# A small projection matrix loaded first, in wider rows on fewer partitions

## The chip, the cores and the metric

The kernel runs on one core of a Trainium2 chip. Times are device microseconds (us) of one execution; a lower time is better. The profile's "span" is what the profiler covers of the same execution; it is some 1.8 us shorter than the time (82.6 against 84.35 us for the kernel before). A run is called slow when it lies over 1.5% above the fastest of the same kernel. Engines: TensorE (PE) multiplies matrices, VectorE (DVE) and GpSimd (POOL) do the elementwise work, ScalarE (ACT) copies and issues DMA, SyncE (SP) only issues DMA.

## The reference

```python
# x: 32 x 512 x 256 f32 (16.8 MB); conditioning: 32 x 64; both projections: 64 x 256
gamma = conditioning @ gamma_proj
beta = conditioning @ beta_proj
return x * (1 + gamma[:, None, :]) + beta[:, None, :]
```

16.8 MB must be read and as much written; gamma and beta need only 136 KB of input.

## The kernel before

x goes through SBUF in four slabs of 4 MB, 32 rows of 1 KB in each of 128 partitions. Each slab is worked on in two pieces of 16 rows: VectorE does 11 rows, GpSimd 5. The small inputs are issued on ACT's queue, x on SP's, the stores on ACT's.

```python
nc.scalar.dma_start(out=cond_s, in_=conditioning)
nc.scalar.dma_start(out=gbproj[:, :dim], in_=gamma_proj)   # 64 partitions, 1 KB rows
nc.scalar.dma_start(out=gbproj[:, dim:], in_=beta_proj)
# SP: slab 0 in two loads (8 and 24 rows), slabs 1 to 3 whole          ...
# cond_T (64 x 512): conditioning transposed, each column 16 times     ...
for s in range(SLABS):
    nc.tensor.matmul(p_t, lhsT=cond_T[:, s*P:(s+1)*P], rhs=gbproj, start=True, stop=True)
    nc.scalar.activation(out=s_t[:, :dim], in_=p_t[:, :dim], ...)      # 1 + gamma, for GpSimd
    nc.scalar.copy(out=s_t[:, dim:], in_=p_t[:, dim:])                 # beta, for GpSimd
for s in range(SLABS):
    for r0 in range(0, ROWS, GROUP):
        # VectorE: v = (gamma + 1) * v, then v + beta; GpSimd: w * gb_s, then w + gb_s   ...
        nc.scalar.dma_start(out=o_v[s, :, r0:r0+GROUP, :], in_=xs[:, r0:r0+GROUP, :])
```

## Time and profile before

| | before |
|---|---|
| time, median of 3 | 84.44 us (84.38 to 84.47) |
| span of the profiled run | 82.6 us |
| conditioning / gamma / beta landed | 3.7 / 10.3 / 14.6 us |
| VectorE's first multiply | 17.5 us |
| first store issued | 25.9 us |
| last load of x landed | 49.5 us |
| VectorE's last operation ends | 66.6 us |
| DMA full | 1.6 to 81.2 us |

A landing time is the issue time plus the "us to landing" of the issue table. Most of the lines behind this table stand in the prediction. Two more follow: the first store in the timeline (start, duration, engine, operation), and the end of the loads among SP's own waits (total, times, longest). SP had issued its last load at 10.6 us, and 38.9 us later x was complete.

```profile
25.94 4.32 ACTq L105 DMA_DIRECT2D out_dram<-xs  x2
...
SPq L132 <- DMA xs<-in_x_dram: 38.9, 1, 38.9
```

### The profile page before, as it was taken

To read this page: it belongs to the slowest core of one execution; us is meant where nothing else is said; L and a number is where in the kernel's file an instruction comes from. 1 tells how busy PE (TensorE), PEld (TensorE's weight loads), DVE (VectorE), ACT (ScalarE), POOL (GpSimd) and SP (SyncE) were. 2 spreads that over 40 slices of the span, in tenths; PEclk is the share of its full clock that TensorE was granted. 3 is DMA by queue.
4 is the path that set the end of the run, shared out by engine and by line. 5 is a ranking of instruction groups with operands and counts; after the bars stand their busy time and mean duration, and the time that the engine had idled before them with its cause. 6 is when DMAs were issued, how large, how long until landed. Compare 5 with 4: busy or idle time off the path is not lost.

```text
span 82.6 us, 156 instructions
## 1 busy us (share of the span) xinstructions
PE 9.1 (11%) x10; PEld 2.8 (3%) x10; DVE 49.9 (60%) x18; ACT 3.9 (5%) x9; POOL 46.2 (56%) x22
## 2 busy tenths in 40 slices
PE   0080000899600000000000000000000000000000
PEld 0100000443000000000000000000000000000000
DVE  2011000059999999999999999999999920000000
ACT  0600000034400000000000000000000000000000
POOL 2000000069999999999999999999995000000000
DMA  3899999969969989998889979899999999999992
GB/s 56 337 508 397 389 397 524 460 302 508 508 270 492 508 381 381 413 476 381 381 381 556 460 302 460 381 468 421 429 452 389 468 421 421 460 389 452 437 421 87
DMA packets 2080, 33.69 MB, mean 408 GB/s; under 512 B 288, under 2 KB 416, under 8 KB 416
## 3 DMA queue, kind: packets, MB, share of 16 engines
q1 hardware_dynamic: 720, 16.78, 48.6%
q10 hardware_dynamic: 1360, 16.92, 48.0%
HBM read 16.92 MB, written 16.78 MB: 408 GB/s over the span
## 4 chain that ended last, share of the span: by engine, by line
DVE 49%; DMA 16%; issue 11%; PE 2%; ACTq 1%; ACT 1%
DVE xs L100 30%; DVE xs L103 19%; DMA gbproj<-in_beta_proj_dram 16%; PE gb_p L79 2%; ACTq L50 1%; ACTq L48 0%; ACT gb_s L82 0%; ACT gb_s L85 0%
## 5 line engine op out<-in xcount | busy, mean ns | idle before, releaser
L102 POOL TENSOR_TENSOR xs<-xs,gb_s 128x1280 f32<-128x1280 f32 x8 | 23.0, 2895 | 16.2 <-ACT gb_s L82 16.2
L100 DVE SCALAR_TENSOR_TENSOR xs<-gb_p,xs 128x2816 f32<-128x2816 f32 x8 | 24.7, 3083 | 10.9 <-ACT gb_s L85 10.9
L103 DVE TENSOR_TENSOR xs<-xs,gb_p 128x2816 f32<-128x2816 f32 x8 | 24.7, 3086 | 0.3
L104 POOL TENSOR_TENSOR xs<-xs,gb_s 128x1280 f32<-128x1280 f32 x8 | 23.0, 2893 | 0.0
L79 PE MATMUL gb_p<-gbproj,cond_T 64*128 64x512 f32 x8 | 7.2, 1074 | 8.9 <-DMA gbproj<-in_beta_proj_dram 8.9
L74 DVE COPY cond_T<-cond_T_p 64x512 f32<-64x512 f32 x1 | 0.7, 683 | 4.3 <-PE cond_T_p L72 4.3
L79 PEld LDWEIGHTS gb_p<-gbproj,cond_T 64*128 64x128 f32 x8 | 2.5, 328 | 13.7 <-issue 13.7
L72 PE MATMUL cond_T_p<-rident,cond_s 32*64 32x512 f32 x2 | 1.9, 1065 | 3.9 <-DMA cond_s<-in_conditioning_dram 3.9
L82 ACT ACTIVATE gb_s<-gb_p 128x256 f32<-128x256 f32 x4 | 1.5, 383 | 16.4 <-PE gb_p L79 16.4
L85 ACT COPY gb_s<-gb_p 128x256 f32<-128x256 f32 x4 | 1.5, 367 | 0.0
L82 ACT ACT_TABLE_LOAD x1 | 1.3, 1283 | 2.4 <-issue 2.4
L67 DVE COPY rident<-ident 32x512 f32<-32x512 f32 x1 | 0.4, 416 | 1.2 <-POOL ident masks.py:199 1.2
L72 PEld LDWEIGHTS cond_T_p<-rident,cond_s 32*64 32x64 f32 x2 | 0.3, 202 | 3.9 <-issue 3.9
masks.py:197 POOL MEMSET ident<- 32x32 f32 x1 | 0.1, 114 | 0.3 <-POOLq L121 0.3
masks.py:199 POOL TENSOR_SCALAR_AFFINE_SELECT ident<-ident 32x32 f32<-32x32 f32 x1 | 0.2, 202 | 0.1
L121 POOL MEMSET const-float32-0.0<- 128x1 f32 x1 | 0.1, 103 | 0.2 <-issue 0.2
L121 POOL MEMSET const-bfloat16-1.0<- 128x1 bf16 x1 | 0.1, 106 | 0.0
L121 POOL MEMSET const-uint8-127<- 128x1 uint8 x1 | 0.1, 106 | 0.0
L121 POOL MEMSET const-float32-1.0<- 128x1 f32 x1 | 0.1, 103 | 0.0
## 6 DMA issues: line engine op xcount, KB each, us to landing
out_dram<-xs ACTq DMA_DIRECT2D x8, 2048.0 KB, 18.2
xs<-in_x_dram SPq DMA_DIRECT2D x3, 4096.0 KB, 32.9
xs<-in_x_dram SPq DMA_DIRECT2D x1, 3072.0 KB, 12.2
xs<-in_x_dram SPq DMA_DIRECT2D x1, 1024.0 KB, 4.6
gbproj<-in_gamma_proj_dram ACTq DMA_DIRECT2D x1, 64.0 KB, 9.1
gbproj<-in_beta_proj_dram ACTq DMA_DIRECT2D x1, 64.0 KB, 12.9
cond_s<-in_conditioning_dram ACTq DMA_DIRECT2D x1, 8.0 KB, 3.0
```

What stands on the lines that cost most here:

```text
L50: nc.scalar.dma_start(out=gbproj[:, :dim], in_=gamma_proj)
L67: nc.vector.tensor_copy(out=rident.rearrange("p (b g) -> p b g", g=REP), in_=ident.to_broadcast([batch, batch, REP]),)
L72: nc.tensor.matmul(cond_T_p, lhsT=cond_s, rhs=rident, start=True, stop=True)
L74: nc.vector.tensor_copy(out=cond_T, in_=cond_T_p)
L79: nc.tensor.matmul(p_t, lhsT=cond_T[:, s * P : (s + 1) * P], rhs=gbproj, start=True, stop=True)
L82: nc.scalar.activation(out=s_t[:, :dim], in_=p_t[:, :dim], func=mybir.ActivationFunctionType.Identity, bias=1.0, scale=1.0)
L85: nc.scalar.copy(out=s_t[:, dim:], in_=p_t[:, dim:])
L100: nc.vector.scalar_tensor_tensor(out=v, in0=rows(g_p, nv), scalar=1.0, in1=v, op0=ALU.add, op1=ALU.mult)
L102: nc.gpsimd.tensor_tensor(out=w, in0=w, in1=rows(g_s, nw), op=ALU.mult)
L103: nc.vector.tensor_add(out=v, in0=v, in1=rows(b_p, nv))
L104: nc.gpsimd.tensor_tensor(out=w, in0=w, in1=rows(b_s, nw), op=ALU.add)
L121: nc = _bacc.Bacc("TRN2", target_bir_lowering=False, num_devices=1)
```

## The change

The intent is an earlier start of VectorE: gamma becomes the first transfer of ACT's queue, as 16 rows of 4 KB and not 64 of 1 KB, with the conditioning and beta behind it. Gamma then lies four rows to a partition, so its product is four accumulated matmuls over 16 partitions, and the conditioning is transposed twice, once for each layout. The elementwise part is also pinned to its written order, so GpSimd no longer does both multiplications of a slab before its additions.

```diff
-    nc.scalar.dma_start(out=cond_s, in_=conditioning)
-    nc.scalar.dma_start(out=gbproj[:, :dim], in_=gamma_proj)
-    nc.scalar.dma_start(out=gbproj[:, dim:], in_=beta_proj)
+    nc.scalar.dma_start(out=gproj, in_=gproj_src)       # "(q j) d -> q j d", 16 x 4 x 256
+    nc.scalar.dma_start(out=cond_s, in_=conditioning)
+    nc.scalar.dma_start(out=bproj, in_=beta_proj)
 ...
-    nc.tensor.matmul(cond_T_p, lhsT=cond_s, rhs=rident, start=True, stop=True)
+    for j in range(CJ):
+        nc.tensor.matmul(cond_T_p[:, j, :], lhsT=cond_s.rearrange("b (q j) -> b j q", j=CJ)[:, j, :],
+                         rhs=ident, start=True, stop=True)
+    nc.tensor.matmul(cond_T_b, lhsT=cond_s, rhs=ident, start=True, stop=True)
 ...   # per slab: two copies that spread the columns, c_t and d_t
-        nc.tensor.matmul(p_t, lhsT=cond_T[:, s * P : (s + 1) * P], rhs=gbproj, start=True, stop=True)
+        for j in range(CJ):
+            nc.tensor.matmul(p_t[:, :dim], lhsT=c_t[:, j, :], rhs=gproj[:, j, :],
+                             start=j == 0, stop=j == CJ - 1)
+        nc.tensor.matmul(p_t[:, dim:], lhsT=d_t, rhs=bproj, start=True, stop=True)
 ...
+    with tc.manual_schedule():
         # the elementwise loop and the stores, as before
```

More of the change, by code (lines that the diff above doesn't have):

```diff
@@ L28 @@
     P = 128
-    SLABS = 4
-    BS = batch // SLABS
-    REP = P // BS
-    ROWS = BS * seq // P
-    assert SLABS * BS == batch and REP * BS == P and ROWS * REP == seq
-    x_v = x.flatten_outer_dims().rearrange("(s p r) d -> s p r d", s=SLABS, p=P)
-    o_v = out.flatten_outer_dims().rearrange("(s p r) d -> s p r d", s=SLABS, p=P)
-    LOADS = {0: [8, 24]}
-    GROUP = 16
-    ON_DVE = 11
+    SLABS = [(8, [8, 24]), (8, [32]), (8, [32]), (8, [32])]
+    assert sum(n for n, _ in SLABS) == batch
+    STORES = [[16, 16], [16, 16], [16, 16], [16, 16]]
+    PIECE, ON_DVE = 16, 11
+    x_f = x.flatten_outer_dims()
+    o_f = out.flatten_outer_dims()
     consts = ctx.enter_context(tc.tile_pool(name="consts", bufs=1))
@@ L44 @@
     psum = ctx.enter_context(tc.tile_pool(name="psum", bufs=1, space=bass.MemoryType.PSUM))
-    cond_s = consts.tile([batch, cond_dim], f32)
-    nc.scalar.dma_start(out=cond_s, in_=conditioning)
-    gbproj = consts.tile([cond_dim, 2 * dim], f32)
-    nc.scalar.dma_start(out=gbproj[:, :dim], in_=gamma_proj)
-    nc.scalar.dma_start(out=gbproj[:, dim:], in_=beta_proj)
-    slabs = []
-    for s in range(SLABS):
-        xs = xpool.tile([P, ROWS, dim], f32, name=f"xs{s}")
-        slabs.append(xs)
-        r = 0
-        for n in LOADS.get(s, [ROWS]):
-            nc.sync.dma_start(out=xs[:, r : r + n, :], in_=x_v[s, :, r : r + n, :])
-            r += n
-        assert r == ROWS
+    slabs = []
@@ new lines, with load @@
+    b0 = 0
+    for s, (n, loads) in enumerate(SLABS):
+        assert P % n == 0
+        rows = n * seq // P
+        r0, r1 = b0 * seq, (b0 + n) * seq
+        slabs.append(dict(
+            n=n, b0=b0, rows=rows, loads=loads,
+            src=x_f[r0:r1, :].rearrange("(p r) d -> p r d", p=P),
+            dst=o_f[r0:r1, :].rearrange("(p r) d -> p r d", p=P),
+            xs=xpool.tile([P, rows, dim], f32, name=f"xs{s}"),
+        ))
+        b0 += n
+    def load(eng, s, i):
+        sl = slabs[s]
+        r = sum(sl["loads"][:i])
+        n = sl["loads"][i]
+        eng.dma_start(out=sl["xs"][:, r : r + n, :], in_=sl["src"][:, r : r + n, :])
@@ new lines @@
+    CP = 16
+    CJ = cond_dim // CP
+    cond_s = consts.tile([batch, cond_dim], f32)
+    gproj = consts.tile([CP, CJ, dim], f32)
+    bproj = consts.tile([cond_dim, dim], f32)
+    gproj_src = gamma_proj.rearrange("(q j) d -> q j d", j=CJ)
+    load(nc.sync, 0, 0)
+    nc.scalar.dma_start(out=gproj, in_=gproj_src)
+    nc.scalar.dma_start(out=cond_s, in_=conditioning)
+    nc.scalar.dma_start(out=bproj, in_=beta_proj)
+    load(nc.sync, 0, 1)
+    load(nc.sync, 1, 0)
+    load(nc.sync, 2, 0)
@@ L64 @@
+    load(nc.sync, 3, 0)
     ident = consts.tile([batch, batch], f32)
     make_identity(nc, ident)
-    rident = consts.tile([batch, batch * REP], f32)
-    nc.vector.tensor_copy(
-        out=rident.rearrange("p (b g) -> p b g", g=REP),
-        in_=ident.to_broadcast([batch, batch, REP]),
-    )
-    cond_T_p = psum.tile([cond_dim, batch * REP], f32)
-    nc.tensor.matmul(cond_T_p, lhsT=cond_s, rhs=rident, start=True, stop=True)
-    cond_T = consts.tile([cond_dim, batch * REP], f32)
-    nc.vector.tensor_copy(out=cond_T, in_=cond_T_p)
@@ L76 @@
-    gb_p, gb_s = [], []
-    for s in range(SLABS):
+    gb_p, gb_s = [], []
+    cond_T_p = psum.tile([CP, CJ, batch], f32)
+    for j in range(CJ):
+        nc.tensor.matmul(cond_T_p[:, j, :],
+                         lhsT=cond_s.rearrange("b (q j) -> b j q", j=CJ)[:, j, :],
+                         rhs=ident, start=True, stop=True)
+    cond_T_b = psum.tile([cond_dim, batch], f32)
+    nc.tensor.matmul(cond_T_b, lhsT=cond_s, rhs=ident, start=True, stop=True)
+    for s, sl in enumerate(slabs):
+        n, b0 = sl["n"], sl["b0"]
+        rep = P // n
+        c_t = consts.tile([CP, CJ, P], f32, name=f"cond_T{s}")
+        nc.vector.tensor_copy(
+            out=c_t.rearrange("q j (b g) -> q j b g", g=rep),
+            in_=cond_T_p[:, :, b0 : b0 + n].to_broadcast([CP, CJ, n, rep]),
+        )
+        d_t = consts.tile([cond_dim, P], f32, name=f"cond_Tb{s}")
+        nc.vector.tensor_copy(
+            out=d_t.rearrange("q (b g) -> q b g", g=rep),
+            in_=cond_T_b[:, b0 : b0 + n].to_broadcast([cond_dim, n, rep]),
+        )
@@ L78 @@
         p_t = psum.tile([P, 2 * dim], f32, name=f"gb_p{s}")
-        nc.tensor.matmul(p_t, lhsT=cond_T[:, s * P : (s + 1) * P], rhs=gbproj,
-                         start=True, stop=True)
+        for j in range(CJ):
+            nc.tensor.matmul(p_t[:, :dim], lhsT=c_t[:, j, :], rhs=gproj[:, j, :],
+                             start=j == 0, stop=j == CJ - 1)
+        nc.tensor.matmul(p_t[:, dim:], lhsT=d_t, rhs=bproj, start=True, stop=True)
         s_t = consts.tile([P, 2 * dim], f32, name=f"gb_s{s}")
@@ L87, with spread @@
         gb_s.append(s_t)
-    def rows(t, n):
+    def spread(t, n):
         return bass.AP(tensor=t.tensor, offset=t.offset, ap=[t.ap[0], [0, n], t.ap[1]])
-    for s in range(SLABS):
-        xs = slabs[s]
-        g_p, b_p = gb_p[s][:, :dim], gb_p[s][:, dim:]
-        g_s, b_s = gb_s[s][:, :dim], gb_s[s][:, dim:]
-        for r0 in range(0, ROWS, GROUP):
-            v = xs[:, r0 : r0 + ON_DVE, :]
-            w = xs[:, r0 + ON_DVE : r0 + GROUP, :]
-            nv, nw = ON_DVE, GROUP - ON_DVE
-            nc.vector.scalar_tensor_tensor(out=v, in0=rows(g_p, nv), scalar=1.0, in1=v,
-                                           op0=ALU.add, op1=ALU.mult)
-            nc.gpsimd.tensor_tensor(out=w, in0=w, in1=rows(g_s, nw), op=ALU.mult)
-            nc.vector.tensor_add(out=v, in0=v, in1=rows(b_p, nv))
-            nc.gpsimd.tensor_tensor(out=w, in0=w, in1=rows(b_s, nw), op=ALU.add)
-            nc.scalar.dma_start(out=o_v[s, :, r0 : r0 + GROUP, :],
-                                in_=xs[:, r0 : r0 + GROUP, :])
+    with tc.manual_schedule():
+        for s, sl in enumerate(slabs):
+            xs = sl["xs"]
+            g_p, b_p = gb_p[s][:, :dim], gb_p[s][:, dim:]
+            g_s, b_s = gb_s[s][:, :dim], gb_s[s][:, dim:]
+            done = 0
+            for n in STORES[s]:
+                for q0 in range(done, done + n, PIECE):
+                    nv, nw = ON_DVE, PIECE - ON_DVE
+                    v = xs[:, q0 : q0 + nv, :]
+                    w = xs[:, q0 + nv : q0 + PIECE, :]
+                    nc.vector.scalar_tensor_tensor(out=v, in0=spread(g_p, nv), scalar=1.0, in1=v,
+                                                   op0=ALU.add, op1=ALU.mult)
+                    nc.gpsimd.tensor_tensor(out=w, in0=w, in1=spread(g_s, nw), op=ALU.mult)
+                    nc.vector.tensor_add(out=v, in0=v, in1=spread(b_p, nv))
+                    nc.gpsimd.tensor_tensor(out=w, in0=w, in1=spread(b_s, nw), op=ALU.add)
+                nc.scalar.dma_start(out=sl["dst"][:, done : done + n, :],
+                                    in_=xs[:, done : done + n, :])
+                done += n
+            assert done == sl["rows"]
 _INS = ['x', 'conditioning', 'gamma_proj', 'beta_proj']
```

## The prediction

> **What bounds the kernel now.** I started with the page's busy shares and 40-slice timeline. No compute engine is near full over the span (VectorE 60%, GpSimd 56%), but the DMA row is.
>
> ```profile
> DVE  2011000059999999999999999999999920000000
> POOL 2000000069999999999999999999995000000000
> DMA  3899999969969989998889979899999999999992
> ...
> DMA packets 2080, 33.69 MB, mean 408 GB/s; under 512 B 288, under 2 KB 416, under 8 KB 416
> ```
>
> VectorE idles for the first eight slices and the last eight; DMA is busy from the second slice to the second last. To see whether the 6s and 8s are gaps or only packets counted where they end, I cut the trace into long stretches. In each row below, the last two numbers are the DMA share and GB/s.
>
> ```profile
> 0.00:1.60 1.60, 0.00 (x0) 0.00 (x0) 0.42 (x1) 0.00 (x0) 0.53 (x6) 1.00 0.00 0
> 1.60:26.00 24.40, 9.09 (x10) 2.79 (x10) 9.13 (x4) 3.87 (x9) 8.70 (x4) 1.00 1.00 417
> 26.00:49.50 23.50, 0.00 (x0) 0.00 (x0) 23.36 (x9) 0.00 (x0) 23.50 (x9) 1.00 1.00 424
> 49.50:81.20 31.70, 0.00 (x0) 0.00 (x0) 16.98 (x6) 0.00 (x0) 13.47 (x5) 1.00 1.00 428
> 81.20:82.60 1.40, 0.00 (x0) 0.00 (x0) 0.00 (x0) 0.00 (x0) 0.00 (x0) 1.00 0.00 0
> ```
>
> Nothing moves for 1.6 us, then all 16 engines are full for 79.6 us (loads alone, loads with stores, stores alone, at nearly one rate), then 1.4 us pass to the end. 1.6 + 79.6 + 1.4 = 82.6, the span. The bytes are the bound.
>
> The chain of waits has to be read with care. It names VectorE and the beta transfer:
>
> ```profile
> DVE 49%; DMA 16%; issue 11%; PE 2%; ACTq 1%; ACT 1%
> DVE xs L100 30%; DVE xs L103 19%; DMA gbproj<-in_beta_proj_dram 16%; PE gb_p L79 2%; ACTq L50 1%; ACTq L48 0%; ACT gb_s L82 0%; ACT gb_s L85 0%
> ```
>
> But these shares add to only 80%: the chain ends with the last VectorE add, at 63.49 + 3.09 = 66.6 us, and 16 us of stores follow it. It shows what delays the first store, not what sets the end.
>
> What the change attacks is real: the waits view has VectorE idle until the conditioning is there, and the issue table has beta, only 64 KB, landing 12.9 us after its issue.
>
> ```profile
> DVE xs L100 <- ACT gb_s L85: 10.9, 1, 10.9
> PE gb_p L79 <- DMA gbproj<-in_beta_proj_dram: 8.9, 1, 8.9
> ```
>
> ```profile
> xs<-in_x_dram SPq DMA_DIRECT2D x1, 3072.0 KB, 12.2
> xs<-in_x_dram SPq DMA_DIRECT2D x1, 1024.0 KB, 4.6
> gbproj<-in_gamma_proj_dram ACTq DMA_DIRECT2D x1, 64.0 KB, 9.1
> gbproj<-in_beta_proj_dram ACTq DMA_DIRECT2D x1, 64.0 KB, 12.9
> cond_s<-in_conditioning_dram ACTq DMA_DIRECT2D x1, 8.0 KB, 3.0
> ```
>
> **What the Trainium skill says.** *DMA: Bandwidth & Descriptors*, section "Where 436 GB/s comes from", gives 435 GB/s as the ceiling of the ports into SBUF. The trace agrees: 417 to 428 GB/s, so at most some 2% to 4% is left inside the full stretch. The same page, "Queues, rings and completion order", says that each DMA engine takes turns between the queues by packet. The trace agrees: between 26 and 50 us, where loads come as 32 KB rows (SP's queue q1) and stores as 16 KB rows (ACT's q10), the shares are 2 to 1:
>
> ```profile
> q1 hardware_dynamic: 238, 6.75, 67.0%
> q10 hardware_dynamic: 224, 3.41, 33.1%
> ```
>
> Its "Issuing engines are not separate DMA queues" says that moving a transfer to another issuer buys no bandwidth; the full stretches agree. *Perfetto Trace Analysis*, "DMA Optimizations", advises against transfers under 2 KB. That is the idea of this change, but in this trace such packets are 0.14 MB of 33.69.
>
> **The change, part by part.**
>
> *Gamma in 4 KB rows, first in ACT's queue.* 64 packets of 1 KB become 16 of 4 KB, one per engine. Gamma landed at 1.17 + 9.1 = 10.3 us, beta at 1.72 + 12.9 = 14.6: 4.35 us for beta's five turns on each engine (four 1 KB rows and one completion), 0.87 us a turn. A 24 KB load row at 428/16 = 26.8 GB/s takes 0.92 us, so each small packet waits behind about one load row. Turns per engine before: conditioning 3, gamma 5, beta 5; after: gamma 2, conditioning 3, beta 5. Three fewer: beta lands near 14.6 - 3 x 0.87 = 12.0 us. The conditioning, once first and there at 3.7 us, is now second; its third turn is the fifth of the queue, where the eighth was over at 10.3, so near 10.3 - 2.6 = 7.7 us. This part is given back.
>
> *Conditioning arithmetic.* Five small transposes (estimate 0.6 us in all, since 512 columns took 1.07 us a pass), then a copy of 16x512 out of PSUM (0.68 us, as its 64x512 kin): 9.0 us. Each slab needs five matmuls of 256 columns in place of one of 512. The instruction order of both builds shows this, and the trace has two records per matmul, so ten. A 512-column record starts every 0.86 us; at half of that, 0.43: 4.3 us a slab where it was 1.7. Gamma of slab 0: 9.0 + 8 x 0.43 = 12.4; beta 0.9 more: 13.3; ScalarE's two copies (0.65 us to the end of the second): 14.0. All four slabs are done by about 27 us, and slab 1 is wanted at 26. The eight PSUM copies on VectorE (about 4 x 0.9 = 3.6 us) fit before 14. Slab 0 itself is there at about 13.3 us (second issue near 1.1, plus 12.2). So VectorE starts near 14 to 14.5 us, not 17.5: 3 us sooner.
>
> *GpSimd order.* The order of both builds shows that GpSimd did multiply, multiply, add, add per slab and will do multiply, add, multiply, add. Before, the first store waited for GpSimd's third operation: 17.30 + 3 x 2.9 = 25.9 us, where VectorE had its half at 23.7. After: two operations, 5.8 us, and VectorE's two, 6.2: 14.3 + 6.2 = 20.5. First store 5.4 us sooner.
>
> *What this does at the end.* Stores that start at 20.5 take a third of the DMA time from loads. By 26 us, 16.78 - 6.75 = 10.0 MB of x had landed; by 20.5 about 2.3 less. The remaining 9.1 MB go at 6.75/23.5 = 0.287 MB/us: loads end near 52, not 49.5. VectorE, at 12.24 us a slab, wants the last slab at 14.3 + 36.7 = 51 and may wait 1 us. It ends near 64.5, not 66.6. Then 1.6 + (same bytes) - 64.5 leaves some 16.5 us of stores queued, instead of 14.5: the gain at the front becomes a longer queue.
>
> *Sum.* The first stretch ran at 417 instead of 428 GB/s: 24.4 x 11/428 = 0.6 us, of which start-up and 24 KB rows are a part; I give the 48 removed packets 0.2. The mixed stretch lost 23.5 x 4/428 = 0.2 us and grows by a third: +0.1. Net -0.1: 84.3 us.
>
> **Rivals.** (1) *The head start is worth its size*: 3 to 5 us less, 80 us. For it: the chain of waits. Against: with 79.6 us of full DMA, 80 in place of 84.4 would need 33.69 MB at over 447 GB/s, above anything in the stretches. (2) *VectorE becomes the bound*: loads are starved by early stores, the last slab comes late, and after 12.2 us of VectorE and 2 MB of store (4.9 us) there are DMA gaps. For it: loads get only two thirds. Against: when loads end at 52, stores of three slabs are released or about to be, 12.6 MB, less some 4.5 MB stored: 8 MB or 19 us of queue against 12.2 us of work. It would need the loads to end after 62 us; that makes 86 or more. (3) *The late conditioning and the extra matmuls eat the head start*: VectorE starts at 16 to 18 us. The time is then 84.4 too. (4) *The small-packet saving is larger*: all of the 0.6 us back: 83.7.
>
> **Range and chances.** Three of the five stories end within 0.2 us of 84.3; start-up of the queues can move it by 0.3 to 0.6 either way: 83.7 to 84.9. A gain of 2% needs 82.75, 1.7 us less than the full DMA stretch allows short of 437 GB/s: 3%. A loss of 2% needs DMA gaps of 1.7 us: 2%.
>
> **What would show it.** Right: DMA share 1.00 from about 1.6 us to 1.4 before the end; packets 2080 - 48 = 2032; beta landing near 12 us, the conditioning near 8; VectorE's first multiply at 14 to 15; first store at 20 to 21; loads ending near 52; VectorE ending at 64 to 65 with the end of the span unmoved. Wrong: an empty DMA slice in the middle or tail (rival 2), or a stretch above 435 GB/s (rival 1).

## The result, and the profile after

The changed kernel took 84.52 us (median of 6 runs, 84.33 to 87.0) against 84.43 us (84.36 to 84.56) in the same rounds. The ratio of the fast runs is 1.0001, with a 95% interval of 0.9987 to 1.0015: no difference. A ratio is the mean time of one kernel's fast runs over that of the other's of the same rounds, so it is not quite the ratio of the medians.

a6 gave a profiled run of 85.04 us. As a single run its state is called unknown; its span of 83.3 us is close to the fast ones (82.5 to 82.8 us), and the lines of the changed kernel are read from it. First its busy rows and packets:

```profile
DVE  0000293199999999999999999999999400000000
POOL 2000000299999999999999999999991000000000
DMA  2899999899989999999999999999999999999980
...
DMA packets 2032, 33.69 MB, mean 405 GB/s; under 512 B 288, under 2 KB 352, under 8 KB 368
```

The packets are the 2,032 that were expected: 48 fewer than before. The long stretches, with DMA share and GB/s last, show the same thing as before: nothing for 1.6 us, full engines, nothing for the last 1.4 us.

```profile
0.00:1.60 1.60, 0.00 (x0) 0.00 (x0) 0.00 (x0) 0.00 (x0) 0.53 (x6) 1.00 0.00 0
1.60:26.00 24.40, 16.21 (x42) 10.31 (x43) 12.84 (x12) 3.20 (x7) 9.70 (x4) 1.00 1.01 414
26.00:51.00 25.00, 4.20 (x10) 2.35 (x8) 24.86 (x9) 0.67 (x3) 24.69 (x9) 1.00 0.99 426
51.00:81.90 30.90, 0.00 (x0) 0.00 (x0) 14.35 (x5) 0.00 (x0) 11.62 (x5) 1.00 0.98 419
81.90:83.30 1.40, 0.00 (x0) 0.00 (x0) 0.00 (x0) 0.00 (x0) 0.00 (x0) 1.00 0.00 0
```

Next the small transfers and the loads' end. The first three lines are the issue table (KB each, us to landing); with issues at 0.74, 1.17 and 1.65 us, gamma was there at 4.6, the conditioning at 9.3 and beta at 14.35 us. The last line is SP's wait, which starts with its last issue at 9.6 us.

```profile
gproj<-in_gamma_proj_dram ACTq DMA_DIRECT2D x1, 64.0 KB, 3.9
bproj<-in_beta_proj_dram ACTq DMA_DIRECT2D x1, 64.0 KB, 12.7
cond_s<-in_conditioning_dram ACTq DMA_DIRECT2D x1, 8.0 KB, 8.1
...
SPq L166 <- DMA xs<-in_x_dram: 38.8, 1, 38.8
```

Last, the front end in the timeline (L87 transposes the conditioning, L107 makes gamma, L109 beta; the second L109 and L111, ScalarE's copy of gamma, belong to the fourth slab; L137 is the first store):

```profile
9.36 0.58 PE L87 MATMUL cond_T_p<-ident,cond_s 32*16 32x32 f32 x8 [9.36 <-DMA cond_s<-in_conditioning_dram]
10.71 3.77 PE L107 MATMUL gb_p<-gproj,cond_T 16*128 16x256 f32 x8 [0.42 <-DVE cond_T L96]
14.44 1.20 PE L109 MATMUL gb_p<-bproj,cond_Tb 64*128 64x256 f32 x2
16.35 3.09 DVE L132 SCALAR_TENSOR_TENSOR xs<-gb_p,xs 128x2816 f32<-128x2816 f32 x1 [3.11 <-ACT gb_s L114]
28.98 1.22 PE L109 MATMUL gb_p<-bproj,cond_Tb 64*128 64x256 f32 x2
30.23 0.39 ACT L111 ACTIVATE gb_s<-gb_p 128x256 f32<-128x256 f32 x1 [4.21 <-PE gb_p L109]
30.38 0.38 ACTq L137 DMA_DIRECT2D out_dram<-xs  x1
```

| | before | after (a6) |
|---|---|---|
| conditioning / gamma / beta landed | 3.7 / 10.3 / 14.6 us | 9.3 / 4.6 / 14.35 us |
| VectorE's first multiply | 17.5 us | 16.35 us |
| first store issued | 25.9 us | 30.4 us |
| last load of x landed | 49.5 us | 48.4 us |
| VectorE's last operation ends | 66.6 us | 65.4 us |

So VectorE started 1.2 us sooner, the first store went out 4.5 us *later*, and the time moved with neither. The first store is later because ACT issues its work in order: the stores stand behind ScalarE's copies for all four slabs, and TensorE, with 4.85 us of matmuls a slab (15.56 to 20.42 us for the second in this trace), delivers the fourth slab only at 30.2 us (28.98 + 1.22). The order on ACT was the same before; there TensorE was done by 22 us and nobody noticed.

Some runs of the changed kernel took 86.8 to 87.1 us, and some of the kernel before 85.8 to 86.2. The slow profile of the changed kernel has the loss in the first half (compare 414 and 426 above).

```profile
1.60:26.00 24.40, 16.26 (x42) 10.32 (x43) 12.85 (x12) 3.21 (x7) 9.71 (x4) 1.00 1.03 392
26.00:49.50 23.50, 4.19 (x10) 2.34 (x8) 23.39 (x8) 0.67 (x3) 23.19 (x9) 1.00 0.97 403
```

### The profile page after: what moved, and what is told of

Read it like the earlier page. It is cut to its first block, busy times and chain, and to the rows that moved or that the text cites. A ratio compares the mean times of both kernels' runs of the same rounds, so it can differ in the third digit from the quotient of the medians.

```text
span 85.2 us, 242 instructions
## 1 busy us (share of the span) xinstructions
PE 20.4 (24%) x50; PEld 12.7 (15%) x50; DVE 52.1 (61%) x24; ACT 3.9 (5%) x9; POOL 46.6 (55%) x22
## 2 busy tenths in 40 slices
DMA packets 2032, 33.69 MB, mean 395 GB/s; under 512 B 288, under 2 KB 352, under 8 KB 368
## 4 chain that ended last, share of the span: by engine, by line
DVE 48%; DMA 15%; issue 10%; PE 1%; ACTq 1%; ACT 1%
DVE xs L132 29%; DVE xs L135 19%; DMA bproj<-in_beta_proj_dram 15%; PE gb_p L109 1%; ACTq L74 1%; ACTq L73 0%; ACT gb_s L111 0%; ACT gb_s L114 0%
## 5 line engine op out<-in xcount | busy, mean ns | idle before, releaser
L134 POOL TENSOR_TENSOR xs<-xs,gb_s 128x1280 f32<-128x1280 f32 x8 | 23.2, 2896 | 15.1 <-ACT gb_s L111 15.0
L107 PE MATMUL gb_p<-gproj,cond_T 16*128 16x256 f32 x32 | 15.1, 649 | 0.4 <-DVE cond_T L96 0.4
L107 PEld LDWEIGHTS gb_p<-gproj,cond_T 16*128 16x128 f32 x32 | 9.9, 325 | 4.8 <-issue 1.9
L96 DVE COPY cond_T<-cond_T_p 16x512 f32<-16x512 f32 x4 | 2.7, 672 | 9.8 <-PE cond_T_p L87 9.8
L109 PE MATMUL gb_p<-bproj,cond_Tb 64*128 64x256 f32 x8 | 4.8, 708 | 0.2 <-DMA bproj<-in_beta_proj_dram 0.2
L87 PE MATMUL cond_T_p<-ident,cond_s 32*16 32x32 f32 x8 | 0.6, 231 | 9.1 <-DMA cond_s<-in_conditioning_dram 9.1
L111 ACT ACTIVATE gb_s<-gb_p 128x256 f32<-128x256 f32 x4 | 1.5, 384 | 24.8 <-PE gb_p L109 24.8
L109 PEld LDWEIGHTS gb_p<-bproj,cond_Tb 64*128 64x128 f32 x8 | 2.0, 308 | 2.8 <-issue 2.2
L87 PEld LDWEIGHTS cond_T_p<-ident,cond_s 32*16 32x16 f32 x8 | 0.4, 117 | 9.1 <-issue 9.1
L101 DVE COPY cond_Tb<-cond_T_b 64x128 f32<-64x128 f32 x4 | 1.1, 269 | 0.0
```

Source lines behind the costliest of these rows:

```text
L87: nc.tensor.matmul(cond_T_p[:, j, :], lhsT=cond_s.rearrange("b (q j) -> b j q", j=CJ)[:, j, :], rhs=ident, start=True, stop=True)
L96: nc.vector.tensor_copy(out=c_t.rearrange("q j (b g) -> q j b g", g=rep), in_=cond_T_p[:, :, b0 : b0 + n].to_broadcast([CP, CJ, n, rep]),)
L101: nc.vector.tensor_copy(out=d_t.rearrange("q (b g) -> q b g", g=rep), in_=cond_T_b[:, b0 : b0 + n].to_broadcast([cond_dim, n, rep]),)
L107: nc.tensor.matmul(p_t[:, :dim], lhsT=c_t[:, j, :], rhs=gproj[:, j, :], start=j == 0, stop=j == CJ - 1)
L109: nc.tensor.matmul(p_t[:, dim:], lhsT=d_t, rhs=bproj, start=True, stop=True)
L111: nc.scalar.activation(out=s_t[:, :dim], in_=p_t[:, :dim], func=mybir.ActivationFunctionType.Identity, bias=1.0, scale=1.0)
```

## The experiments

Two theories were set against each other: *the bytes are the bound* (the DMA engines are full, VectorE's start has slack) and *the head start counts* (the chain through conditioning and VectorE sets the end). All outputs were correct.

**a1: the changed kernel again.** No edit.

> The changed kernel again, for a profile in the fast state (the first profile was of a slow run, 87.0 us). Theory (the bytes are the bound): 84.3 to 84.6 us, ratio to the kernel before within 0.3%, DMA share 1.00 from 1.6 us to 1.4 us before the end; the first store is issued near 29 to 30 us, later than the 25.9 us of before, because ACT issues it after its copies of all four slabs, and TensorE is not done with the fourth slab before 29 us. Rival (the wait for the conditioning is worth its size): VectorE starts about 1 to 3 us sooner than 17.5 us and the time falls by as much, to 81.5 to 83.5.

Measured: 84.81 us median (84.31 to 86.86), ratio 1.0027 (0.9997 to 1.0058). The profile was slow again (86.86 us). The time fits the bytes.

**a2: the first store made early.** ScalarE's copies are issued one slab ahead of the stores.

```diff
-        nc.scalar.activation(out=s_t[:, :dim], ...)      # in the matmul loop, all four slabs
-        nc.scalar.copy(out=s_t[:, dim:], ...)
+    side_copies(0)
+    for s, sl in enumerate(slabs):
+        if s + 1 < len(slabs):
+            side_copies(s + 1)
         # elementwise work and stores of slab s
```

> The changed kernel with ACT's copies issued one slab ahead of the stores, not all four slabs ahead, so that the first store goes out when its data is done (near 22 us in place of 30). Theory (the bytes are the bound): the first store moves by some 8 us and the time by less than 0.4 us: 84.0 to 84.8. Rival (the late first store ate a gain that the head start would have given): 80 to 82.5 us.

Measured: 84.77 us (84.45 to 85.84), ratio 1.0029 (1.0002 to 1.0057); the profiled run was fast, 84.45 us. Its timeline has the first stores here:

```profile
22.39 6.49 ACTq L142 DMA_DIRECT2D out_dram<-xs  x2
```

Eight us sooner than in the changed kernel, 3.5 us sooner than before, and no gain at all. Where the head start went is seen at the other end: VectorE finished at 65.2 us, and the DMA engines were full until the same 1.4 us before the end (stretches of this run):

```profile
26.00:51.50 25.50, 3.95 (x9) 2.16 (x7) 25.36 (x9) 1.29 (x4) 24.58 (x9) 1.00 1.00 427
51.50:81.30 29.80, 0.00 (x0) 0.00 (x0) 13.61 (x5) 0.00 (x0) 11.53 (x4) 1.00 1.00 427
81.30:82.70 1.40, 0.00 (x0) 0.00 (x0) 0.00 (x0) 0.00 (x0) 0.00 (x0) 1.00 0.00 0
```

**a3: 2 MB that nobody waits for.**

```diff
     load(nc.sync, 3, 0)
+    extra = xpool.tile([P, 16, dim], f32, name="extra")
+    nc.sync.dma_start(out=extra, in_=slabs[3]["src"][:, :16, :])
```

> The changed kernel with 2 MB of x loaded a second time into a tile that nobody reads; nothing waits for it on any compute engine. Theory (the bytes are the bound): 2.10 MB at 0.428 MB per us, 4.9 us more: 89.0 to 89.7. Rival (the chain through the conditioning and VectorE sets the end, the queue has room): 84.4 to 85.5.

Measured: 89.7 and 89.9 us in the fast runs, 91.9 in the two slow ones. The five fast runs of a1 beside it average 84.71 us, so the 2.10 MB cost 5.1 us, 0.41 MB per us, slightly more than expected. No compute engine did anything more or later for it. The rival, that the queue has room, falls.

**b1 and b2: how much VectorE's start is worth.** The kernel before in written order, with the small loads on SP's queue behind slab 1 (b1) or slab 2 (b2).

```diff
-    nc.scalar.dma_start(out=cond_s, in_=conditioning)   # and gamma, beta
 for s in range(SLABS):
     ...   # loads of slab s
+    if s == 1:                                          # b2: s == 2
+        nc.sync.dma_start(out=cond_s, in_=conditioning) # and gamma, beta
```

> The kernel before, in written order, with the three small loads on SP's queue behind slab 1, so that VectorE starts near 26 us, 8 to 9 us later than in the kernel before. Theory (the bytes are the bound; VectorE has slack of the 14.6 us of stores still queued when it ends at 66.6, less 4.9 us for its last store, 9.7 us): within 1%, 84.2 to 85.3. Rival (VectorE's start counts one for one): 92 to 94 us.

Measured: 86.77 us (86.57 to 86.88), ratio 1.0269 (1.024 to 1.0297). Outside what either theory expected, but near the first. VectorE started at 28.75 us, later than the 26 assumed: the transposes and their copy, 2.6 us that lay beside a wait before, now came after the landing. That is 11.2 us later than before, for 2.3 us of time. In its timeline VectorE ends at 77.8 us, and the span, 85.0, is 7.2 us longer:

```profile
28.75 3.09 DVE L102 SCALAR_TENSOR_TENSOR xs<-gb_p,xs 128x2816 f32<-128x2816 f32 x1 [2.84 <-ACT gb_s L86]
...
74.74 3.09 DVE L105 TENSOR_TENSOR xs<-xs,gb_p 128x2816 f32<-128x2816 f32 x1
77.91 0.34 ACTq L107 DMA_DIRECT2D out_dram<-xs  x1
```

So the tail after VectorE is 7.2 us, not the 6.3 that the expectation used (4.9 + 1.4), and the slack before was 82.6 - 66.6 - 7.2 = 8.8 us. A delay of 11.2 against that slack gives 2.4; measured, 2.3. With this correction b2 was written down ahead of its run:

> As b1_small_after_slab1, with the small loads behind slab 2. In b1 VectorE started at 28.75 us and the span ended 7.2 us after VectorE's last operation. Theory (the time is the longer of the full DMA stretch and VectorE's start plus 49.0 plus 7.2 us): the small loads land near 33, VectorE starts near 38.4, span 38.4 + 49.0 + 7.2 = 94.6, time 96 to 97, with a DMA gap between the end of the loads near 42 us and the first store. Rival (the DMA queue absorbs this as well): below 90 us.

Measured: 96.45 us (96.38 to 96.56), ratio 1.1415 (1.1396 to 1.1434); span 94.6 us, to the tenth; VectorE started at 38.38 us. Here the other bound rules, and the DMA engines do show a gap, in the stretch between the loads and the first stores (VectorE's start from the timeline, then three stretches):

```profile
38.38 3.09 DVE L102 SCALAR_TENSOR_TENSOR xs<-gb_p,xs 128x2816 f32<-128x2816 f32 x1 [2.84 <-ACT gb_s L86]
...
1.60:41.80 40.20, 8.14 (x10) 2.79 (x10) 4.07 (x3) 2.37 (x7) 3.55 (x2) 1.00 1.00 421
41.80:46.00 4.20, 0.99 (x2) 0.00 (x0) 4.20 (x2) 0.65 (x2) 4.20 (x2) 1.00 0.15 62
46.00:93.20 47.20, 0.00 (x0) 0.00 (x0) 41.21 (x14) 0.00 (x0) 38.25 (x14) 1.00 0.82 350
```

The two together give a rule for this kernel: the span is the longer of the span with full DMA (82.6 us) and VectorE's start + 49.0 (VectorE's work) + 7.2 us (the tail). The tail was taken from b1; b2 tested the rule. By it the kernel before stood 8.8 us inside the first; an earlier start only widens that.

**b3: GpSimd's order alone.**

```diff
+    ctx.enter_context(tc.manual_schedule())
     for s in range(SLABS):
         xs = slabs[s]
```

> The kernel before with one part of the change alone: GpSimd's operations in written order (multiply, add, multiply, add). Theory (the bytes are the bound): the first store goes out at 23.8 us, when VectorE is done, in place of 25.9, and the time stays within 0.4%: 84.1 to 84.8. Rival (the first store's time counts): 82.3 us.

Measured: 84.61 us (84.52 to 85.7), ratio 1.0032 (0.9985 to 1.0078). The profiled run was the one of 85.7 us, so only its order is read from it: the first store went out at 24.0 us, as expected. This part of the change moves the first store by 2 us and the time by nothing that can be seen.

**b4: the order of the small loads alone, in 1 KB rows.** The kernel before with gamma first, conditioning second, beta third.

```diff
-    nc.scalar.dma_start(out=cond_s, in_=conditioning)
     nc.scalar.dma_start(out=gbproj[:, :dim], in_=gamma_proj)
+    nc.scalar.dma_start(out=cond_s, in_=conditioning)
     nc.scalar.dma_start(out=gbproj[:, dim:], in_=beta_proj)
```

> The kernel before with gamma issued first, conditioning second, beta third, all still in 1 KB rows (64 packets for gamma, not 16). It tells what the 4 KB rows alone buy in the changed kernel, where the conditioning landed at 9.0 and beta at 13.95 us. Turn theory of the prediction (every small packet costs a turn of 0.87 us wherever it stands): three turns more than the changed kernel, so conditioning at 11.6 and beta at 14.6 to 16.5. Rival (gamma's packets in first place pass during the start, when the load rows are 8 KB, and the second transfer starts no sooner than 5.5 us anyway): conditioning within 0.7 us of 9.0, beta within 0.7 us of 14. Time 84.2 to 84.9 by both.

Measured: 84.68 us (84.53 to 86.1), ratio 1.0015 (0.9996 to 1.0035). Its issue table, with issues at 0.75, 1.95 and 1.31 us:

```profile
gbproj<-in_gamma_proj_dram ACTq DMA_DIRECT2D x1, 64.0 KB, 5.2
gbproj<-in_beta_proj_dram ACTq DMA_DIRECT2D x1, 64.0 KB, 11.7
cond_s<-in_conditioning_dram ACTq DMA_DIRECT2D x1, 8.0 KB, 7.4
```

Gamma was there at 5.95 us, the conditioning at 8.7 and beta at 13.65, the last two no later than in the changed kernel (9.3 and 14.35). The rival holds for the first place in the queue, and the turn theory (each small packet delays those behind it by 0.87 us, wherever it stands) falls there: 64 rows of 1 KB delayed those behind them no more than 16 of 4 KB did. Of this run's packets on ACT's queue, 80 passed between 4.6 and 5.6 us, beside 39 of the loads. In the kernel before, with gamma second, they went one for one with the load rows (packets, MB, share between 5 and 10.5 us; q1 is SP's queue, q10 ACT's):

```profile
q1 hardware_dynamic: 83, 2.02, 87.0%
q10 hardware_dynamic: 82, 0.07, 3.7%
```

In first place the wider rows brought gamma itself 1.3 us sooner, and nothing else. VectorE started at 16.55 us here, with the old matmuls: the order alone gave 1.0 of the changed kernel's 1.2 us.

**a4: the changed kernel with the conditioning first.**

```diff
-    nc.scalar.dma_start(out=gproj, in_=gproj_src)
     nc.scalar.dma_start(out=cond_s, in_=conditioning)
+    nc.scalar.dma_start(out=gproj, in_=gproj_src)
     nc.scalar.dma_start(out=bproj, in_=beta_proj)
```

> The changed kernel with the conditioning issued first and gamma in 4 KB rows second. It tells what set VectorE's start at 16.1 us in the changed kernel: there gamma's matmuls for slab 0 ended at 14.2 us, just after beta landed at 13.95. Theory (beta's landing alone holds it once the conditioning is early): conditioning near 3.7 us, gamma's matmuls done by 12, beta within 0.7 us of 13.95, VectorE at 15.6 to 16.4. Rival (the late conditioning was what cost): VectorE at 14 us or sooner. Time 84.3 to 84.9 by both, because 2 us at VectorE's start lie within its slack.

Measured: 84.71 us (84.31 to 86.62), ratio 1.003 (1.001 to 1.0049). The profile is of a slow run, so its front is read with care: beta at 13.05 us, VectorE at 15.1, between the two expectations. TensorE waited for beta alone:

```profile
13.18 1.19 PE L109 MATMUL gb_p<-bproj,cond_Tb 64*128 64x256 f32 x2 [1.41 <-DMA bproj<-in_beta_proj_dram]
```

In the changed kernel no such wait stands before this instruction, because gamma's matmuls end at the same moment. So both the late conditioning and beta held VectorE there. How much belongs to each can't be told from a slow run.

Beside the kernel before, which has the same order in 1 KB rows, this run shows what the wide rows do in second place. Its issue table has

```profile
gproj<-in_gamma_proj_dram ACTq DMA_DIRECT2D x1, 64.0 KB, 6.7
```

so gamma was there at 1.17 + 6.7 = 7.9 us, not 10.3. That is 2.4 us sooner, near the 2.6 of three turns, and beta came 1.55 us sooner. Less GB/s can hardly be what brought them forward. So, as far as a slow run can tell, the turns count in second place, though not in first.

**a5: the changed kernel a third time.** No edit.

> The changed kernel a third time, for a fast profile: four of four profiled executions so far fell in the slow state and nine of nine others at 84.3 to 84.9 us did not. Theory (the slow state is chance, with the bytes as the bound): 84.3 to 84.9 us when fast. If the profile is fast: VectorE's first multiply at 16.1 us, first store near 30.1, DMA share 1.00. If it is slow again: 86.8 to 87.1, with loads alone below 400 GB/s.

Measured: 84.36 us in the one fast run, 86.91 to 87.12 in the other three, two of them without a profile.

**c1: the slack spent.** If the start has slack, it can be traded for larger rows: slab 0 in one load, slabs 0 to 2 stored whole, in written order.

```diff
-    LOADS = {0: [8, 24]}
+    LOADS = {}
 ...   # one store per slab for slabs 0 to 2, two for slab 3
```

> The kernel before in written order, its head start spent instead of lengthened: slab 0 in one load of 32 KB rows, and slabs 0 to 2 stored whole, in 32 KB rows; only the last slab is stored in two halves. VectorE starts some 2 to 3 us later (near 20) and the first store goes out near 32 us. Theory (the bytes are the bound, VectorE has 8.8 us of slack): no loss, and at most what the first stretch lacked, 0.6 us: 83.7 to 84.6. Rival (start and first store count): 87 us or more.

Measured: 84.71 us (84.55 to 84.86), ratio 1.0027 (1.0013 to 1.004). VectorE started at 21.64 us and the first store went out at 34.06 us,

```profile
34.06 0.37 ACTq L110 DMA_DIRECT2D out_dram<-xs  x1
```

4.1 and 8.1 us later than before, at a cost of 0.3%. The rival (87 us or more) falls a second time. But it was no gain either: the first stretch ran at 414 GB/s, no faster than with the smaller rows, so the 0.6 us hoped for there was not to be had in this way.

**a6: one look for a profile of the changed kernel.** No edit.

> The changed kernel once more, one look for a profile in the fast state; no question of cause hangs on it. If fast (84.3 to 84.9 us): DMA share 1.00 from 1.6 us to 1.4 us before the end, some 414 GB/s up to 26 us, VectorE's first multiply near 16.1 and the first store near 30.1 us. If slow again (86.8 to 87.2 us): loads alone below 395 GB/s up to 26 us, the stores alone at 430.

Measured: 85.04 us; its profile is the one shown in the result.

No version beat the kernel before.

## Why the prediction was right or wrong

The time was right: 84.52 us, where 84.3 was predicted, in a range of 83.7 to 84.9. The reason given for it was right too and is shown by runs: full DMA in every stretch between 1.6 us and 1.4 us before the end (a2, a6), extra bytes paid for at 0.41 MB per us (a3), first stores from 22.4 us (a2) to 34.1 us (c1) with times within 0.3% of the kernel before. The net -0.1 us of the sum is too small for these runs to tell. Of its rivals, "the head start is worth its size" and "the small-packet saving is larger" did not happen; "VectorE becomes the bound" happened only where it was forced (b1, b2). The third rival, that the late conditioning and the extra matmuls eat most of the head start, is the one that happened: VectorE started at 16.35 us, inside its 16 to 18, a head start of 1.2 us and not 3.

Several steps on the way were wrong, and the bound hid it:

- *"Three fewer: beta lands near 12.0 us", conditioning "near 7.7".* They landed at 14.35 and 9.3 us. The step charged every small packet a turn of 0.87 us wherever it stands. b4 shows that gamma's packets in first place cost those behind them nothing that wider rows would save; in second place they did (a4, a slow run).
- *"0.43: 4.3 us a slab ... All four slabs are done by about 27 us."* The records came at 0.47 us (eight in 3.77), a slab took 4.85 us, and with the late start the fourth was done at 30.2.
- *"First store 5.4 us sooner."* It was 4.5 us later. The step looked at the data and not at the queue: the stores wait on ACT behind the copies of the fourth slab. a2 moves those copies and gets the store out at 22.4 us. This is the largest error, and worth nothing in time.
- *"Loads end near 52", "VectorE ends near 64.5".* The first followed from the store and fell with it: 48.4 us. Where the store did go out early, in a2, the loads ended at 51.5 us (last issue 9.3 + 42.2 of wait), so that step itself held. The second was 65.4.
- *The slack.* The prediction gave no figure for it and argued from queued bytes (14.5 us of stores at VectorE's end). By the rule from b1 and b2, a late VectorE is free for 8.8 us, because the last store can't start before it and the span ends 7.2 us later.
- *"Short of 437 GB/s".* A sum: 33.69 MB in 79.6 - 1.7 = 77.9 us is 432 GB/s, not 437. It bears only on the 3% given to a gain.

The sum gave the removed packets 0.2 us. No run shows such a gain: the first stretch of a2 and of a6 ran at 414 GB/s, against 417 before.

## What to carry to other kernels

Read the full stretches of the DMA before the chain of waits: a chain that ends 16 us before the span ends explains the start of the work, not its end. Before shortening a wait, lengthen it: one run with a late VectorE (b1), checked by a second (b2), told that VectorE could have started up to 8.8 us later for nothing. At 4.1 us later (c1) the cost was 0.3%. And when an operation is made earlier, look at what stands ahead of its successor in the issuing engine's own order, as the stores here stood behind four slabs of copies.

## What the Trainium skill lacked or had wrong

- *DMA: Bandwidth & Descriptors*, "Queues, rings and completion order", says that an engine drains a whole packet of one queue before it turns to the next, and gives 9 to 17 descriptors as a typical packet. In these traces a counted packet is one row of up to 32 KB: SP's 720 packets before are 640 rows of x and 80 completions (five loads, 16 each). A turn let one such row by: between 5 and 10.5 us in the kernel before, 83 packets of the loads and 82 small ones passed, one for one.
- The same page gives no figure for what the place of a small load in its queue costs beside a bulk load. Here the first of three landed after 3.0 us (8 KB, before), 3.9 us (64 KB in 4 KB rows, a6) or 5.2 us (64 KB in 1 KB rows, b4), while the 8 KB conditioning, moved to second place, took 8.1 us (a6).
- *Perfetto Trace Analysis*, "DMA Optimizations", says that small DMAs, under 2 KB, have much overhead and that batching them can raise throughput greatly. It doesn't say whether rows of a larger transfer count. Here wider rows brought gamma sooner, by 1.3 us in first place and 2.4 us in second (a4, slow), but not the end: 84.68 us with 1 KB rows (b4), 84.52 us with 4 KB rows (the changed kernel). Before, all rows of 1 KB or less held 0.14 of 33.69 MB.
- No page read describes the slow runs: one core, a granted clock of 1.00 throughout, and loads at 392 instead of 414 GB/s up to 26 us.
